# A state-space layer's decay rows: one tile of 32 partitions, copied to DRAM one group of heads at a time

## The chip, the cores and the metric

The kernel runs on one core of one Trainium2 chip. The metric is device time in microseconds (us); lower is better. The core has five engines with queues of their own, each of which takes its instructions in order: PE (matmuls), ACT (activations, copies), DVE (elementwise work), POOL (here masks and small adds) and SP, which issues nearly all DMAs.

## The reference

Two layers. Each is a half-step feed-forward part, a mixer, and a second half-step feed-forward part, with a layer norm behind each. The mixer of layer 0 is a bidirectional state-space scan over 512 tokens with 32 heads in 4 groups (8 heads of 64 channels each, state size 128); that of layer 1 is differential attention. The scan is what the change touches. In one direction, by chunks:

```python
def ssd_chunked(X, dt, A, Bm, Cm):
    Xc = (X * dt[..., None]).reshape(b, c, CHUNK, g, j, p)
    a = (dt * A).reshape(b, c, CHUNK, g, j).transpose(0, 3, 4, 1, 2)
    a_cs = jnp.cumsum(a, axis=-1)
    L = jnp.exp(segsum(a))                     # decay between two tokens of a chunk
    CB = jnp.einsum('bclgn,bcsgn->bgcls', Cc, Bc)
    y_diag = jnp.einsum('bgcls,bgjcls,bcsgjp->bclgjp', CB, L, Xc)
    ...
    y_off = jnp.einsum('bclgn,bcgjpn,bgjcl->bclgjp', Cc, states, jnp.exp(a_cs))
    return (y_diag + y_off).reshape(b, t, h, p)
```

For every head and direction this needs the cumulated decay of each token, once with tokens along the partitions (as the bias of an activation) and once with tokens along the free axis, the same row on all 128 partitions.

## The kernel before, in words

All matrices are float32, held as a rounded part and a rest (`hi`, `lo`), so that each product is three matmuls (`mm3`, line 176). Weights come from DRAM in units of 512 KB (`load`, line 99, four `raw` buffers in this layer), ACT rounds a unit (line 123), DVE takes the rest (line 124), and 24 matmuls of 128x512 use it. PE has work for nearly the whole span.

`ssm` (line 651) runs the state-space layer. It first projects group 0 (`win`: two units for B and C, four for x, four for z). Among these stands `dt_chain` (line 673), which makes the step sizes and cumulated decays of all heads: PE turns the cumulated values `cs` (tokens on partitions) into rows, one per head and direction, with four transposes of 64 columns (line 720), so that forward heads lie on partitions 0 to 31 and backward heads on 32 to 63 of one PSUM tile. ACT copies all 64 into `rows` (line 722) and writes the exponentials of one half of each direction to `rowe` (lines 724, 725).

A row must reach 128 partitions. That goes by way of DRAM: four DMAs on SP (line 729) write `rows` and `rowe` to `scr`, every row 16 times over (16 copies x 32 heads x 3 kinds x 512 tokens, 3.1 MB). Then, per head, `ssd_head` (line 819) reads them back with each of the 16 copies going to 8 partitions: `rw` (line 823, both directions' decays, 512 KB, two buffers) and `ch` (line 825, the exponentials, 256 KB, three buffers). POOL masks `rw` with four instructions per head (line 840). `ssd_mats` (line 845) then makes a head's decay matrix for one half of the tokens: four exponentials on ACT (lines 848 to 851), an add on POOL (854), a product on DVE (855). `ssd_out` (line 858) multiplies with it on PE (line 865).

The loop of a group (line 932) has 8 steps, here called s0 to s7: a pair of heads (0 and 1, 2 and 3, ...) times two halves of the tokens. A "block" below is the six matmul instructions of one step. Between steps stand units of the next group's projections, so that PE has something to do. `prepare(1)` (line 778; its first instruction on PE is line 783) follows group 0's last step.

The order on each queue is not that of the code: a scheduler places each instruction by its own estimate of when its inputs are there, so a change of a DMA's shape can move instructions on all engines. An instruction that has to wait stops what is behind it on its queue.

Of the kernel before, what the change touches and what calls it, by code (L numbers as in the profile page):

```python
# [9 lines left out]
F32 = mybir.dt.float32  # L10
F32R = mybir.dt.float32r
AF = mybir.ActivationFunctionType
ALU = mybir.AluOpType

P = 128
T = 512
# [6 lines left out]
NG = 4  # L23
# [23 lines left out]
def hybrid_trunk(tc, xT, cb, par, cst, adaw, wgu, wdn0, wdn1, wdn2, wdt, win, wso, wqk, wv, wao, dist_in, dtp, lam_in, out):  # L47
    nc = tc.nc
# [13 lines left out]
    def big(dt=F32, name="big"):  # L62
        return ap.tile([P, T], dt, tag="a", name=name)
# [4 lines left out]
    def acc(tag="acc"):  # L68
        return ps.tile([P, T], F32, tag=tag, name=tag, bufs=BANKS[tag])
# [7 lines left out]
    ident, ones = csts[:, 0, :], csts[:, 1, :]  # L77
# [573 lines left out]
    def ssm(n):  # L651
        u = next_u[0]
        sc = ExitStack()
        ep = sc.enter_context(tc.tile_pool(name="ep", bufs=2))
        dp = sc.enter_context(tc.tile_pool(name="dp", bufs=1, space=bass.MemoryType.DRAM))
# [5 lines left out]
        W = 256  # L661
        bias = ep.tile([P, 4, 64], F32, name="ssbias", bufs=1)
        dd = ep.tile([P, 4, 32], F32, name="dd", bufs=1)
        scr = dp.tile([16, 32, 3, T], F32, name="scr")

        def dt_proj():
            w = split(load(wdt, 512))
# [5 lines left out]
        def dt_chain(pd):  # L673
            dtT = tmp("dtT")
            nc.scalar.activation(dtT[:64], pd[:64], AF.Copy)
            pt = acc("ln")
            for i in range(4):
                nc.tensor.transpose(pt[:, i * 64 : (i + 1) * 64], dtT[:64, i * P : (i + 1) * P], ident[:64, :64])
            e1, e2, e3 = (ep.tile([P, T], F32, tag="E", name="E", bufs=NE) for _ in range(3))
            v, q, e, uu, lu = e1[:, :W], e1[:, W:], e2[:, :W], e2[:, W:], e3[:, :W]  # L680
            nc.vector.tensor_tensor(out=v, in0=pt[:, :W], in1=dtc[:, :W], op=ALU.add)
            nc.vector.scalar_tensor_tensor(out=q, in0=v, scalar=-1.0, in1=v, op0=ALU.mult, op1=ALU.max)
            nc.scalar.activation(e, q, AF.Exp, scale=-1.0)
            ea = e3[:, W:]
            nc.scalar.activation(ea, dtc[:, W:], AF.Exp)
            nc.vector.tensor_scalar(out=v, in0=v, scalar1=0.0, scalar2=None, op0=ALU.max)
            nc.vector.tensor_scalar(out=uu, in0=e, scalar1=1.0, scalar2=None, op0=ALU.add)
            nc.scalar.activation(lu, uu, AF.Ln)
            nc.vector.tensor_scalar(out=uu, in0=uu, scalar1=1.0, scalar2=None, op0=ALU.subtract)
            nc.vector.tensor_tensor(out=uu, in0=e, in1=uu, op=ALU.subtract)  # L690
            nc.vector.tensor_scalar(out=e, in0=e, scalar1=-0.5, scalar2=1.0, op0=ALU.mult, op1=ALU.add)
            nc.vector.tensor_tensor(out=uu, in0=uu, in1=e, op=ALU.mult)
            nc.vector.tensor_tensor(out=lu, in0=lu, in1=uu, op=ALU.add)
            nc.vector.tensor_tensor(out=v, in0=v, in1=lu, op=ALU.add)
            at = q
            nc.vector.scalar_tensor_tensor(out=at, in0=v, scalar=-1.0, in1=ea, op0=ALU.mult, op1=ALU.mult)
            nc.vector.tensor_scalar(out=v, in0=v, scalar1=1e-37, scalar2=None, op0=ALU.max)
            nc.scalar.activation(lu, v, AF.Ln)
            pcs = acc("ln")
            nones = tmp("nones")[:, :P]  # L700
            nc.gpsimd.memset(nones, -1.0)
            plan = {
                (0, 0): [(sgt, 0), (nones, 1)], (0, 1): [(sgt, 1)],
                (0, 2): [(sle, 2)], (0, 3): [(ones, 2), (sle, 3)],
                (1, 0): [(sge, 0), (ones, 1)], (1, 1): [(sge, 1)],
                (1, 2): [(slt, 2)], (1, 3): [(nones, 2), (slt, 3)],
            }
            for (dr, i), lst in plan.items():
                for k, (mk, j) in enumerate(lst):
                    nc.tensor.matmul(  # L710
                        pcs[:, i * 64 + dr * 32 : i * 64 + dr * 32 + 32], lhsT=mk,
                        rhs=at[:, j * 64 + dr * 32 : j * 64 + dr * 32 + 32],
                        start=k == 0, stop=k == len(lst) - 1,
                    )
            cs = tmp("cs")[:, :W]
            nc.scalar.activation(cs, pcs[:, :W], AF.Copy)
            nc.vector.tensor_tensor(out=bias.rearrange("p i h -> p (i h)"), in0=lu, in1=cs, op=ALU.subtract)
            pr = acc("ln")
            for i in range(4):
                nc.tensor.transpose(pr[:64, i * P : (i + 1) * P], cs[:, i * 64 : (i + 1) * 64], ident)  # L720
            rows = big(name="rows")
            nc.scalar.activation(rows[:64], pr[:64], AF.Copy)
            rowe = big(name="rowe")
            nc.scalar.activation(rowe[32:64, :W], pr[32:64, :W], AF.Exp)
            nc.scalar.activation(rowe[0:32, W:], pr[0:32, W:], AF.Exp)
            nc.scalar.activation(dd[:, 0:2, :], bias[:, 0:2, 0:32], AF.Exp)
            nc.scalar.activation(dd[:, 2:4, :], bias[:, 2:4, 32:64], AF.Exp)
            for j, a, b, src in ((0, 0, T, rows[0:32]), (1, 0, T, rows[32:64]), (2, 0, W, rowe[32:64]), (2, W, T, rowe[0:32])):
                nc.sync.dma_start(
                    scr[:, :, j, a:b].rearrange("r h x -> h r x"), src[:, a:b].unsqueeze(1).broadcast_to([32, 16, b - a])  # L730
                )

        last_in, last_exp = [None], [None]

# [83 lines left out]

        def ssd_head(h, Ct):

            src = scr[:, h].unsqueeze(1)
            rw = ep.tile([P, 2, T], F32, tag="rw", name="rw")
            nc.sync.dma_start(rw, src[:, :, 0:2].broadcast_to([16, 8, 2, T]))
            ch = ep.tile([P, T], F32, tag="ch", name="ch", bufs=3)
            nc.sync.dma_start(ch, src[:, :, 2].broadcast_to([16, 8, T]))
            nc.vector.tensor_tensor(out=ch, in0=ch, in1=Ct, op=ALU.mult)
            dx = ep.tile([P, 2, 2, P], F32, tag="dx", name="dx")
            f4 = rw[:, 0, :].rearrange("p (c o q) -> p c o q", c=2, o=2)
            b4 = rw[:, 1, :].rearrange("p (c o q) -> p c o q", c=2, o=2)
            for o, i_, fwd in (  # L830
                (f4[:, :, 0, :], f4[:, :, 0, :], True), (b4[:, :, 1, :], b4[:, :, 1, :], False),
            ):
                mask(o, i_, fwd)
            for o in range(2):
                mask(dx[:, :, o, :], (b4 if o == 0 else f4)[:, :, o, :], o == 1, inplace=False)
            return rw, ch, dx
# [75 lines left out]
        ln, shifting = LN(n), []  # L912
# [11 lines left out]
        for g in range(NG):  # L924
            xt, cbs, states, Ct = cur
            nbc, nxs = [], []
            first = units_z(g, zs[g])[len(zs[g]) :]
            if g < NG - 1:
                first = units_bc(g + 1, nbc) + units_x(g + 1, nxs) + first
            todo = first + ([lambda gg=g - 1: outp(gg)] * 4 if g > 0 else [])  # L930
            tot, done, batched = len(todo), 0, False
            for s in range(8):
                pr_, c = divmod(s, 2)
                ft = g * 4 + pr_
                if c == 0:
                    heads = [ssd_head(ft * 2 + hh, Ct) for hh in range(2)]
                    py = acc("mid")
                mats = [ssd_mats(ft * 2 + hh, c, heads[hh][0], heads[hh][2], cbs) for hh in range(2)]
                ssd_out(pr_, c, py, mats, [hd[1] for hd in heads], xt, states)
                if c == 1:  # L940
                    nc.vector.scalar_tensor_tensor(
                        out=xs[pr_], in0=xs[pr_], scalar=pc(C_D + ft), in1=py, op0=ALU.mult, op1=ALU.add
                    )
                if s == 0 and norm is not None:
                    rest = norm()
                if s == 2 and norm is not None:
                    yrs[g - 1] = rest()
                while done < tot - (2 if g == NG - 1 else 0) and done < (s + 1) * tot // 8:
                    todo[done]()
                    done += 1  # L950
                if done >= len(first) and not batched and (s >= 6 or done == tot):
                    batched = True
                    silu(zs[g] + nbc + nxs)
                    if g < NG - 1:
                        cur = prepare(g + 1, nxs, nbc)
            norm = (lambda g=g, xs=xs: gated_norm(g, xs, zs[g]))
            xs = nxs
# [314 lines left out]
```

## Time and profile before

| what | value |
|---|---|
| three runs | 2177.52, 2182.35, 2185.12 us (median 2182.35) |
| the profiled execution | 2177.95 us |
| its span, first to last instruction | 2176.1 us |
| mean granted TensorE clock | 0.992 |
| busy share of PE, DVE, ACT, POOL | 97%, 81%, 50%, 7% |
| state-space layer, from the decay chain on | about 400 to 780 us |
| the four writes of `scr` | issued 416.7 to 419.9 us |
| first step's first block on PE | 459.6 us |
| `prepare(1)` on PE | 512.6 us |

The profile gives times from the first instruction. A line of a timeline reads: start, length, engine, source line, operation, what it writes and reads, how many, and in square brackets how long the engine was idle before it and what ended that. "DMA to landing" is the time from a DMA's issue to its last byte's arrival. A window's row lists busy time per engine, then the granted TensorE clock, the busy share of the 16 DMA engines, and GB/s moved. [...]

### The profile page before, as it was taken

What the parts mean: (1) busy time and instruction counts of PE and PEld (TensorE: products, weight loads), DVE (VectorE), ACT (ScalarE), POOL (GpSimd) and SP (SyncE); (2) the same over time, 40 slices, a digit from 0 to 9 for tenths busy, and PEclk for the clock granted to TensorE, in tenths of its full rate; (3) what the DMA queues carried; (4) which work ended last, traced back from release to release, by engine and by line L of the source; (5) the groups of instructions that cost most, each with busy time, mean ns of one, the idle gap of its engine ahead of it and who ended that gap; (6) DMA issues with size and microseconds to landing.
All of it is one profiled execution on the core that took longest, in us unless ns stands there. A gap on an engine that the chain in (4) does not pass through costs nothing.

```text
span 2176.1 us, 34041 instructions
## 1 busy us (share of the span) xinstructions
PE 2120.5 (97%) x13206; PEld 1857.6 (85%) x13206; DVE 1765.4 (81%) x2934; ACT 1092.2 (50%) x1828; POOL 155.2 (7%) x258
## 2 busy tenths in 40 slices
PE   7999999999999998999999999999999999999997
PEld 6889899866777677989899989899988878989897
DVE  6979998556666688979988998997777888958696
ACT  4424354757656546434355534344766647524353
POOL 0000000034332310000000000000111100000000
PEclk9999999999999998999999999999999999999999
DMA  8853644464445413554533272733322212423231
GB/s 320 304 213 118 222 130 166 115 181 136 145 126 158 123 64 126 174 185 153 196 125 112 95 265 92 254 100 124 89 78 78 88 44 84 136 70 116 77 117 40
DMA packets 90082, 301.19 MB, mean 138 GB/s; under 512 B 10048, under 2 KB 13504, under 8 KB 89920
## 3 DMA queue, kind: packets, MB, share of 16 engines
q1 hardware_dynamic: 88384, 294.81, 41.3%
q0 software_dynamic: 1536, 4.20, 0.9%
q8 instruction: 104, 1.70, 0.3%
q14 instruction: 58, 0.48, 0.1%
HBM read 289.53 MB, written 5.24 MB: 135 GB/s over the span
## 4 chain that ended last, share of the span: by engine, by line
PE 84%; DVE 5%; issue 4%; ACT 3%; POOL 2%; DMA 2%; POOLq 0%; SPq 0%; ACTq 0%; DVEq 0%
PE acc L176 67%; PE mid L176 10%; PE mid L865 2%; DMA raw<-in_adaw 1%; PE mid L1033 1%; DVE raw L195 1%; POOL E L854 1%; PE ln L176 1%; PE ln L813 1%; DMA raw<-in_wdn 0%; ACT wh L123 0%; ACT p L1043 0%; PE ln L1055 0%; POOL dx L840 0%; PE ln L264 0%
## 5 line engine op out<-in xcount | busy, mean ns | idle before, releaser
L176 PE MATMUL acc<-hi,wh 128*128 128x256 f32 (+1 forms) x1576 | 526.9, 336 | 3.1 <-ACT hi L153 1.9
L176 PE MATMUL acc<-hi,wl 128*128 128x256 f32 (+1 forms) x1576 | 525.9, 334 | 0.0
L176 PE MATMUL acc<-lo,wh 128*128 128x256 f32 (+1 forms) x1576 | 525.6, 334 | 0.3 <-DVE lo L154 0.2
L176 PE MATMUL acc<-uh,wh 128*128 128x256 f32 (+1 forms) x1160 | 391.8, 338 | 0.2 <-ACT wh L123 0.2
L176 PE MATMUL acc<-ul,wh 128*128 128x256 f32 (+1 forms) x1160 | 390.5, 337 | 0.0
L176 PE MATMUL acc<-uh,wl 128*128 128x256 f32 (+1 forms) x1160 | 389.5, 336 | 0.0
L123 ACT ACTIVATE wh<-raw 128x1024 fp32r<-128x1024 f32 (+1 forms) x210 | 213.0, 1022 | 272.7 <-DMA raw<-in_wdn 95.9
L528 ACT ACTIVATE wh<-raw 128x1024 fp32r<-128x1024 f32 x198 | 209.1, 1059 | 254.1 <-DVE raw L538 121.8
L176 PEld LDWEIGHTS acc<-hi,wh 128*128 128x128 f32 x1576 | 297.9, 189 | 40.1 <-ACT hi L153 5.2
L176 PEld LDWEIGHTS acc<-lo,wh 128*128 128x128 f32 x1576 | 298.0, 189 | 31.8 <-DVE lo L154 1.9
L176 PEld LDWEIGHTS acc<-hi,wl 128*128 128x128 f32 x1576 | 298.0, 189 | 29.9 <-issue 0.5
L124 DVE TENSOR_TENSOR wl<-raw,wh 128x1024 fp32r<-128x1024 f32 (+1 forms) x210 | 248.0, 1184 | 47.6 <-ACT wh L123 46.7
L529 DVE TENSOR_TENSOR wl<-raw,wh 128x1024 fp32r<-128x1024 f32 x198 | 241.2, 1220 | 24.0 <-ACT wh L528 23.0
L176 PEld LDWEIGHTS acc<-uh,wh 128*128 128x128 f32 x1160 | 219.3, 189 | 29.6 <-issue 6.6
L176 PEld LDWEIGHTS acc<-ul,wh 128*128 128x128 f32 x1160 | 219.7, 189 | 24.9 <-issue 3.3
L176 PEld LDWEIGHTS acc<-uh,wl 128*128 128x128 f32 x1160 | 219.7, 189 | 23.9 <-issue 2.4
L538 DVE TENSOR_TENSOR raw<-raw 128x512 f32<-128x512 f32 x264 | 181.3, 689 | 4.7
L195 DVE SCALAR_TENSOR_TENSOR raw<-raw,cond 128x1024 f32<-128x1024 f32 x144 | 174.1, 1221 | 9.6 <-DMA raw<-in_adaw 9.4
L401 DVE SCALAR_TENSOR_TENSOR resid<-acc,gv,resid 128x512 f32<-128x512 f32 (+1 forms) x164 | 108.6, 667 | 71.1 <-PE acc L176 70.8
L341 POOL TENSOR_TENSOR rr<-vr,mhalf 128x2 f32<-128x2 f32 x12 | 9.5, 789 | 1512.9 <-DVE vr L337 1512.9
L176 PE MATMUL mid<-uh,wh 128*128 128x256 f32 (+2 forms) x332 | 99.6, 302 | 0.6 <-DVE up L570 0.6
L176 PE MATMUL mid<-uh,wl 128*128 128x256 f32 (+2 forms) x332 | 99.3, 299 | 0.0
(267 smaller groups left out, 3939.6 us busy)
## 6 DMA issues: line engine op xcount, KB each, us to landing
raw<-in_wgu SPq DMA_DIRECT2D x176, 512.0 KB, 4.0
raw<-in_adaw SPq DMA_DIRECT2D x144, 512.0 KB, 4.7
raw<-in_wdn SPq DMA_DIRECT2D x64, 448.0 KB, 4.0
raw<-in_win SPq DMA_DIRECT2D x40, 512.0 KB, 3.8
raw<-in_wdn SPq DMA_DIRECT2D x32, 512.0 KB, 4.7
rw<-scr SPq DMA_DIRECT2D x32, 512.0 KB, 5.5
ch<-scr SPq DMA_DIRECT2D x32, 256.0 KB, 3.6
raw<-in_wso SPq DMA_DIRECT2D x16, 512.0 KB, 3.6
```

Of the source, the lines that this page charges most:

```text
L123: nc.scalar.activation(hi[:, :n], raw, AF.Copy)
L124: nc.vector.tensor_tensor(out=lo[:, :n], in0=raw, in1=hi[:, :n].bitcast(F32), op=ALU.subtract)
L176: last = nc.tensor.matmul(o, lhsT=a, rhs=b, start=start and j == 0, stop=j == n - 1, skip_group_check=not start)
L195: nc.vector.scalar_tensor_tensor(out=raw, in0=raw, scalar=1.0, in1=cond, op0=ALU.mult, op1=ALU.mult, accum_out=mods[l][:, j : j + 1],)
L401: nc.vector.scalar_tensor_tensor(out=res[d][:, a:b], in0=pd[:, a:b], scalar=gvec[n][:, d : d + 1], in1=res[d][:, a:b], op0=ALU.mult, op1=A ...
L528: nc.scalar.activation(x[0], r, AF.Copy)
L529: nc.vector.tensor_tensor(out=x[1], in0=r, in1=x[0].bitcast(F32), op=ALU.subtract)
L538: nc.vector.tensor_tensor(out=o, in0=x, in1=y, op=ALU.add)
L813: nc.tensor.matmul(pst, lhsT=bt[:, i * P : (i + 1) * P], rhs=xd, start=o == 0, stop=o == 1)
L854: nc.gpsimd.tensor_tensor(out=dg, in0=dg, in1=dx[:, c], op=ALU.add)
L865: nc.tensor.matmul(py[hh * 64 : (hh + 1) * 64, cc], lhsT=lhs, rhs=rhs, start=k == 0, stop=k == 2)
L1033: nc.tensor.matmul(ss[m], lhsT=q[:, c], rhs=qks[h, 1][m], start=j == 0, stop=j == 1)
```

## The change

The rows go to one tile of 32 partitions, `rows` with head on the partition and three kinds of 512 along the free axis. For that, each direction is transposed by itself (eight transposes of 32 columns into two PSUM tiles), ACT copies the forward rows, DVE the backward ones, and ACT writes the exponentials into the third part. `scr` becomes four DRAM tiles of 16 x 8 x 3 x 512, one per group of eight heads, and each is written by one DMA whose source is the eight partitions of that group (`copy_rows`, 128 runs of 6 KB, 786 KB). The first copy is issued in `dt_chain`; those of groups 1, 2 and 3 are issued in group 0's loop, behind the reads of the first, second and third pair of heads. The bytes are the same in all.

```diff
-        scr = dp.tile([16, 32, 3, T], F32, name="scr")
+        scr = [dp.tile([16, 8, 3, T], F32, name=f"scr{g}") for g in range(NG)]
+        rows = ep.tile([32, 3, T], F32, name="rows", bufs=1)
...
-            pr = acc("ln")
-            for i in range(4):
-                nc.tensor.transpose(pr[:64, i * P : (i + 1) * P], cs[:, i * 64 : (i + 1) * 64], ident)
-            rows = big(name="rows")
-            nc.scalar.activation(rows[:64], pr[:64], AF.Copy)
-            rowe = big(name="rowe")
-            nc.scalar.activation(rowe[32:64, :W], pr[32:64, :W], AF.Exp)
-            nc.scalar.activation(rowe[0:32, W:], pr[0:32, W:], AF.Exp)
+            pr = [acc("ln") for _ in range(2)]
+            for dr in range(2):
+                for i in range(4):
+                    c = i * 64 + dr * 32
+                    nc.tensor.transpose(pr[dr][:32, i * P : (i + 1) * P], cs[:, c : c + 32], ident)
+            nc.scalar.activation(rows[:, 0, :], pr[0][:32], AF.Copy)
+            nc.vector.tensor_copy(rows[:, 1, :], pr[1][:32])
+            nc.scalar.activation(rows[:, 2, :W], pr[1][:32, :W], AF.Exp)
+            nc.scalar.activation(rows[:, 2, W:], pr[0][:32, W:], AF.Exp)
+            copy_rows(0)
...
-            for j, a, b, src in ((0, 0, T, rows[0:32]), (1, 0, T, rows[32:64]), (2, 0, W, rowe[32:64]), (2, W, T, rowe[0:32])):
-                nc.sync.dma_start(
-                    scr[:, :, j, a:b].rearrange("r h x -> h r x"), src[:, a:b].unsqueeze(1).broadcast_to([32, 16, b - a])
-                )
+        def copy_rows(g):
+            src = rows[g * 8 : (g + 1) * 8].rearrange("h j x -> h (j x)").unsqueeze(1)
+            nc.sync.dma_start(scr[g].rearrange("r h j x -> h r (j x)"), src.broadcast_to([8, 16, 3 * T]))
...
-            src = scr[:, h].unsqueeze(1)
+            src = scr[h // 8][:, h % 8].unsqueeze(1)
...
                     heads = [ssd_head(ft * 2 + hh, Ct) for hh in range(2)]
+                    if g == 0 and pr_ < NG - 1:
+                        copy_rows(pr_ + 1)
```

The scheduler's order changes with it. On SP, at the place where the rows are written and the first heads read, before (all copies of `scr` have one name; `rw` and `ch` are one head's reads, and the number tells the buffer's use):

```order
L729 DMA scr_3721<-rows_4070 32x16x512 x2
L729 DMA scr_3721<-rowe_4072 32x16x256 x2
L823 DMA rw_4294<-scr_3721 128x1x1024
L823 DMA rw_4312<-scr_3721 128x1x1024
L825 DMA ch_4296<-scr_3721 128x1x512
L825 DMA ch_4314<-scr_3721 128x1x512
L825 DMA ch_4444<-scr_3721 128x1x512
```

and, in the changed kernel, from the same place on (`scr0` to `scr3` are the four groups' tiles; the lines moved by three or five):

```order
L734 DMA scr0_3721<-rows_3725 8x16x1536
L734 DMA scr1_3722<-rows_3725 8x16x1536
L826 DMA rw_4299<-scr0_3721 128x1x1024
L828 DMA ch_4301<-scr0_3721 128x1x512
L826 DMA rw_4317<-scr0_3721 128x1x1024
L828 DMA ch_4319<-scr0_3721 128x1x512
L828 DMA ch_4450<-scr0_3721 128x1x512
L734 DMA scr2_3723<-rows_3725 8x16x1536
L826 DMA rw_4448<-scr0_3721 128x1x1024
L826 DMA rw_4466<-scr0_3721 128x1x1024
L828 DMA ch_4468<-scr0_3721 128x1x512
L828 DMA ch_4599<-scr0_3721 128x1x512
```

Group 1's copy stands ahead of the first read, group 2's ahead of the reads of heads 2 and 3. Behind the last row shown come group 3's copy, the `rw` reads of heads 4 and 5, one more `ch`, and only then the next weight units; before, three weight units stood right behind the last row shown.

On PE, at the end of step s1 in group 0 (line 865 before is 868 now; `mid` is the step pair's output, `E` a decay matrix, `acc` a projection), before:

```order
L865 MATMUL mid_4330<-ch_4296,st_4269 64x256
L865 MATMUL mid_4330<-ch_4314,st_4269 64x256
L176 MATMUL acc_4653<-uh_3534,wh_4649 128x512
L176 MATMUL acc_4653<-ul_3535,wh_4649 128x512
L176 MATMUL acc_4653<-uh_3534,wl_4650 128x512
```

and in the changed kernel at the same place:

```order
L868 MATMUL mid_4336<-ch_4301,st_4274 64x256
L868 MATMUL mid_4336<-ch_4319,st_4274 64x256
L868 MATMUL mid_4485<-E_4486,xt_4259 64x256
L868 MATMUL mid_4485<-E_4493,xt_4259 64x256
L868 MATMUL mid_4485<-E_4486,xt_4269 64x256
L868 MATMUL mid_4485<-E_4493,xt_4269 64x256
L868 MATMUL mid_4485<-ch_4450,st_4297 64x256
```

Where a projection stood behind s1, the next step's block stands now. The blocks of s0 to s4 follow each other without a projection between them. The 120 projection matmuls that stood between s1 and `prepare(1)` all stand behind s4: 24, s5, 24, s6, 24, s7, 48. Ahead of s0 nothing moved but the transposes.

## The prediction

> **What bounds the kernel now.** I read the page first, then PE's waits within the state-space layer, then PE's and SP's timelines around the place of the change, then the DMA rate there.
>
> ```profile
> PE 2120.5 (97%) x13206; PEld 1857.6 (85%) x13206; DVE 1765.4 (81%) x2934; ACT 1092.2 (50%) x1828; POOL 155.2 (7%) x258
> L123 ACT ACTIVATE wh<-raw 128x1024 fp32r<-128x1024 f32 (+1 forms) x210 | 213.0, 1022 | 272.7 <-DMA raw<-in_wdn 95.9
> L124 DVE TENSOR_TENSOR wl<-raw,wh 128x1024 fp32r<-128x1024 f32 (+1 forms) x210 | 248.0, 1184 | 47.6 <-ACT wh L123 46.7
> ```
>
> PE is busy for 97% of the span, so a change counts only by what it does to PE. The two rows under it are the splitting of a weight unit, 1.02 us on ACT and 1.18 on DVE. In the layer's loop (440 to 770 us), the longest entry among PE's waits is this one:
>
> ```profile
> PE mid L865 <- DVE E L855: 4.9, 2, 4.5
> ```
>
> 4.9 us in two waits. PE's timeline shows where, with the last projection ahead of s0, the blocks of s0 and s1, the first part of the block of s4, and `prepare(1)`:
>
> ```profile
> 458.11 0.39 PE L176 MATMUL acc<-uh,wh 128*128 128x512 f32 x1
> 458.34 0.39 PE L176 MATMUL acc<-ul,wh 128*128 128x512 f32 x1
> 459.56 1.08 PE L865 MATMUL mid<-E,xt 128*64 128x256 f32 x8
> 461.77 0.60 PE L865 MATMUL mid<-ch,st 128*64 128x256 f32 x4
> ...
> 478.10 0.39 PE L176 MATMUL acc<-uh,wh 128*128 128x512 f32 x1
> 483.00 1.08 PE L865 MATMUL mid<-E,xt 128*64 128x256 f32 x2 [4.51 <-DVE E L855]
> ...
> 512.64 0.66 PE L783 MATMUL ln<-csts,xc 128*128 128x128 f32 x4
> ```
>
> Projection matmuls follow each other every 0.23 us (458.11, 458.34), so the 120 between s1 and `prepare(1)` take 27.6 us. The blocks of s0 and s1 together run from 459.56 to 462.1, 1.3 us each. The one large stall is ahead of s4: PE has nothing from 478.5 to 483.0. What it costs beyond the 4.5 us is in the window's clock:
>
> ```profile
> 480.00:500.00 20.00, 16.86 (x66) 9.41 (x66) 13.50 (x19) 12.94 (x31) 11.03 (x19) 0.83 0.53 151
> ```
>
> 0.83 of the full clock over 20 us is 3.4 us lost. So the stall is worth about 8 us in all, and that is the most the change could win here.
>
> The stall comes by way of SP. Its queue, then the time to landing of the reads of head 2 (issued 450.6) and of heads 4 and 5 (465.7 and 466.3):
>
> ```profile
> 416.74 0.87 SPq L729 DMA_DIRECT2D scr<-rows  x2
> 417.65 4.64 SPq L729 DMA_DIRECT2D scr<-rowe  x2
> 428.88 2.99 SPq L823 DMA_DIRECT2D rw<-scr  x2
> 434.71 1.80 SPq L825 DMA_DIRECT2D ch<-scr  x3
> 436.56 2.67 SPq L99 DMA_DIRECT2D raw<-in_win  x3
> ...
> 463.61 1.92 SPq L99 DMA_DIRECT2D raw<-in_win  x3
> 465.69 1.63 SPq L823 DMA_DIRECT2D rw<-scr  x2
> ```
>
> ```profile
> L823 SPq DMA_DIRECT2D rw<-scr x1: 521/521/521, 450.6 to 450.6; - x1
> DMA to landing us min/median/max: 5.1/5.1/5.1
> L823 SPq DMA_DIRECT2D rw<-scr x2: 521/762/1003, 465.7 to 466.3; - x2
> DMA to landing us min/median/max: 12.0/12.5/13.1
> ```
>
> A read alone lands in 5.1 us; behind three weight units it takes 12.0 and 13.1. Head 5's landed at 466.3 + 13.1 = 479.4, and PE began s4 3.6 us later. Reads are served behind what was issued ahead of them on the queue. That matters most for this change, since it puts the copies of later groups ahead of reads.
>
> **The change part by part.** *Small edits.* The rows that bear on them:
>
> ```profile
> 414.98 1.05 PE L720 MATMUL ln<-csts,cs 128*64 128x128 f32 x4
> 417.14 0.37 ACT L725 ACTIVATE rowe<-ln 32x256 f32<-32x256 f32 x1
> 446.14 0.51 ACT L848 ACTIVATE E<-rw,ssbias 128x256 f32<-128x256 f32 x1
> 440.34 0.77 POOL L840 TENSOR_SCALAR_AFFINE_SELECT rw<-rw 128x256 f32<-128x256 f32 x2 [1.21 <-DMA rw<-scr]
> ```
>
> Eight transposes stand for four; the four took 1.05 us on PE, and half the columns may halve each, so between 0 and 1.05 us is added on PE's path: 0.5. ACT does the same three row writes (the last ended at 417.5), and DVE takes one copy of 512 columns, by ACT's 0.37 for 256 about 0.74 us; both lie beside projections. Were that cover gone, they would delay the first DMA by 0.7 us. `rows` being ready sets the first copy's issue: 417.6.
>
> *Earlier reads.* In the SP timeline the first `rw` is issued at 428.9, after the two writes of `rows`, and the first `ch` at 434.7. A first copy that lands sooner would bring these forward. It buys nothing by itself: head 1's first mask began at 440.34, and ACT started s0's exponentials only at 446.14, when it was through with `prepare(0)`; PE came to s0 at 459.56.
>
> *The copies.* This is the term that decides. How long does one copy take whose source is 8 partitions? The first old write, 1.05 MB from 32 partitions, by its landing, and the rates while writes of 2 KB runs (421 to 427), of 1 KB runs (427 to 431), reads alone (435 to 437) and weights (443 to 445) filled the queue, and while the kernel's last result went to DRAM from 128 partitions in 1 KB runs:
>
> ```profile
> L729 SPq DMA_DIRECT2D scr<-rows x1: 334/334/334, 416.7 to 416.7; - x1
> DMA to landing us min/median/max: 6.7/6.7/6.7
> ```
>
> ```profile
> 421.00:427.00 6.00, 6.00 (x29) 4.95 (x28) 2.41 (x4) 4.82 (x8) 0.00 (x0) 1.00 0.99 197
> 427.00:431.00 4.00, 4.00 (x21) 3.21 (x19) 1.99 (x3) 1.54 (x3) 0.00 (x0) 1.00 0.98 189
> 435.00:437.00 2.00, 2.00 (x13) 1.45 (x11) 0.69 (x1) 0.60 (x1) 0.00 (x0) 1.00 1.04 240
> 443.00:445.00 2.00, 2.00 (x9) 1.27 (x8) 1.74 (x3) 0.99 (x3) 0.00 (x0) 1.00 1.01 403
> 2172.00:2174.00 2.00, 0.00 (x0) 0.00 (x0) 0.19 (x1) 0.78 (x2) 0.00 (x0) 0.50 0.96 323
> ```
>
> All 16 DMA engines were busy in each (0.96 to 1.04), yet the rate is 197, 189, 240, 403 and 323 GB/s. Halving the run cost only 4%; going to DRAM isn't the limit either, since 128 partitions did 323. What the slow rows share is a source of 32 partitions. If the rate follows the partitions, 8 give a quarter, 49 GB/s, and a copy of 0.786 MB takes T = 16 us. The other end is the rate kept: T = 4 us. From 128 to 32 partitions the rate fell by 1.7, not by 4, and 1.7 once more would make T = 7; but 323 and 403 from as many partitions show that something else caps these, while at 32 partitions the run length hardly moved the rate. So I take 16, from the row nearest to the case (197, 2 KB runs, 32 partitions, the same target).
>
> [...]
>
> *The queue.* Before rw of head 5 can land, the new order puts on SP's queue all four copies, six `rw` and five `ch`. Sizes and landing of these and of a weight unit:
>
> ```profile
> rw<-scr SPq DMA_DIRECT2D x32, 512.0 KB, 5.5
> ch<-scr SPq DMA_DIRECT2D x32, 256.0 KB, 3.6
> raw<-in_win SPq DMA_DIRECT2D x40, 512.0 KB, 3.8
> ```
>
> That is 6 x 0.524 + 5 x 0.262 = 4.46 MB of reads: 18.6 us at the 240 GB/s of reads alone, 11.1 at the 403 of weights; I take 15. Four copies are 64. The landing of the first write leaves a fixed part of 6.7 - 1.05 MB/197 GB/s = 1.4. Their waits (for buffers, that is for ACT and PE on earlier heads) fall inside the time that the queue is still at work on a copy, so head 5 lands at X = 417.6 + 64 + 15 + 1.4 = 498.0.
>
> *What that does to PE.* The five blocks s0 to s4 stand together, so from s1 on PE has only blocks until head 5 is there. As before, s4 starts 3.6 us after the landing, and its block at a cold clock takes about twice 1.2: it ends at X + 6. Weights aren't late: their units are issued behind head 5's read, land about 3.8 us after it and want 1.02 + 1.18 of splitting, so the first is ready at about X + 6 too. Then 120 projection matmuls (27.6) and three blocks (3.9), and a cold clock's 3.4 again: `prepare(1)` starts at X + 41, against 512.6 before. So the change costs X - 471.6 = 26.4, and 0.5 for the transposes: 27. Behind `prepare(1)` no copy is left and PE is as full as it was; I book nothing there.
>
> Of the two waits above, the 4.5 us and its cold clock are not lost twice: they are in the 512.6.
>
> **Rivals.** *The copy isn't slow* (T up to 9). Then copies don't bind: head 4's and 5's reads are issued about when they were (after the exponentials of heads 2 and 3), now with no weight units ahead, and land in 5.1 us: X = 466.3 + 5.1 = 471.4, and the change costs 0.3. PE idles between the blocks instead of ahead of s4 alone, and gets it back behind s4. For it: full DMA engines at 189 and 197 might mean a limit of the engines, or of a source row sent 16 times, which would not scale with partitions. Against: 323 from 128 partitions. By the profiled execution 2178, by the median 2182. [...]
>
> *Faster.* With T = 4 the first copy lands at 423, the whole chain of heads moves up with it, and s4 is ready before PE gets there. Then the stall goes with its clock: -8, 2170. It decides if head 5 lands by about 466. Against: ACT's 446.14, which no copy moves.
>
> *The order alone costs.* Copies are fast, but weights behind head 5's read come after s4, and PE waits for them at a cold clock: 8 us at most by the stall it has now, 2186.
>
> *The change doesn't do what it says*: "behind the first reads" holds for groups 2 and 3 only; group 1's copy is ahead of the first read on SP. That is in the sum already.
>
> **How the numbers follow.** The sum stands against the profiled execution's 2177.95 us: 2177.95 + 27 = 2205. The median shown is 4.4 above that execution; half of this puts the forecast at 2207. Chances: slow copy 0.72, copy not slow 0.17, faster 0.05, order alone 0.05, something else 0.01. With T from 12 to 18 and reads of 11 to 18.6, X goes from 478 to 509.6, the cost from 7 to 38.5, the time from 2185 to 2221: the forecast's own range. 8 in 10 need part of the second case, so the low end goes to 2179, the high end to 2222. A measurement can tell about 0.3% (6.5 us) from no change: faster by more, 0.06; within, 0.16 (nearly all of the second case, a little of the fourth); slower, 0.78.
>
> **What would show it.** Right: the first copy lands 16 to 18 us after its issue, GB/s in 418 to 434 about 50, the first `rw` is issued at about 435, PE idles between blocks from 462 to 500, `prepare(1)` starts near 539, and the distance from there to the end is as before. Wrong: a copy that lands in under 11 us; reads that overtake copies (landing in 5 us while a copy is under way); `prepare(1)` before 520; or time given back behind it.

## The result, and the profile after

| | before | changed |
|---|---|---|
| median of the runs, us | 2179.93 (2176.78 to 2185.12, 4 runs) | 2202.66 (2197.85 to 2203.89, 4 runs) |
| profiled execution, us | 2177.95 | 2197.85 |
| its span, us | 2176.1 | 2196.1 |

The ratio is 1.0102, with a 95% interval of 1.0085 to 1.0119: the change costs about 22 us. The forecast was 2207.

The first line of the page to read is the busy time, since a change counts by what PE does.

```profile
PE 2119.8 (97%) x13210; PEld 1859.5 (85%) x13210; DVE 1768.3 (81%) x2935; ACT 1093.1 (50%) x1828; POOL 158.1 (7%) x258
```

PE's 2119.8 us of work are the 2120.5 of before; the span has grown by 20.0, so all of it is idle time. PE's waits between 400 and 800 us name it (line, what it waited for: us in total, times, longest), and PE's timeline shows where it lies. `E` is a decay matrix, made from a head's `rw`; L786 is `prepare(1)`, and L778 the batch of SiLU activations on ACT that writes the `xc` which `prepare(1)` reads.

```profile
PE mid L868 <- DVE E L858: 22.4, 4, 11.6
PE ln L786 <- ACT xc L778: 4.9, 1, 4.9
```

```profile
459.86 1.08 PE L868 MATMUL mid<-E,xt 128*64 128x256 f32 x8
...
475.21 1.12 PE L868 MATMUL mid<-E,xt 128*64 128x256 f32 x2 [11.56 <-DVE E L858]
...
492.37 2.05 PE L868 MATMUL mid<-E,xt 128*64 128x256 f32 x7 [10.04 <-DVE E L858]
...
494.52 1.17 PE L868 MATMUL mid<-ch,st 128*64 128x256 f32 x3
...
533.22 0.93 PE L786 MATMUL ln<-csts,xc 128*128 128x128 f32 x4 [4.90 <-ACT xc L778]
```

s0 starts when it did (459.86 against 459.56). Then there are holes of 11.6 us ahead of s2 and 10.0 ahead of s4, where before had one of 4.5, and a new one of 4.9 ahead of `prepare(1)`. That starts at 533.2 in place of 512.6, 20.6 us later, so all of the loss has come about by here. From there to the end of the span it is 1662.9 us, before 1663.5: nothing is given back.

The holes come from SP's queue. Its timeline (start, time of issuing, line), then the rate in four stretches (the last three columns are the granted clock, the busy share of the 16 DMA engines, and GB/s), then the landing of the reads of heads 4 and 5:

```profile
418.13 0.66 SPq L734 DMA_DIRECT2D scr<-rows  x2
434.87 0.63 SPq L826 DMA_DIRECT2D rw<-scr  x1
435.54 4.94 SPq L828 DMA_DIRECT2D ch<-scr  x1
...
449.23 0.48 SPq L734 DMA_DIRECT2D scr<-rows  x1
458.21 5.44 SPq L826 DMA_DIRECT2D rw<-scr  x2
...
466.90 0.48 SPq L734 DMA_DIRECT2D scr<-rows  x1
475.20 5.44 SPq L826 DMA_DIRECT2D rw<-scr  x2
```

```profile
422.00:426.00 4.00, 4.00 (x20) 3.30 (x19) 1.38 (x2) 3.28 (x7) 0.00 (x0) 1.00 0.47 49
430.00:434.00 4.00, 4.00 (x23) 3.27 (x22) 2.27 (x3) 2.97 (x5) 0.00 (x0) 1.00 0.46 49
...
436.00:438.00 2.00, 1.95 (x11) 1.22 (x9) 0.69 (x1) 0.58 (x1) 0.00 (x0) 1.00 0.90 179
438.00:440.00 2.00, 2.00 (x10) 1.46 (x9) 0.36 (x1) 1.09 (x2) 0.00 (x0) 1.00 0.49 53
```

```profile
L826 SPq DMA_DIRECT2D rw<-scr x2: 514/2432/4349, 475.2 to 476.3; - x2
DMA to landing us min/median/max: 11.1/11.6/12.0
```

A copy alone moves 49 GB/s, 16 us for its 0.786 MB, and the first `rw`, which waits for it, is issued 16.7 us behind it. The busy share of the 16 engines is 0.47 meanwhile, 7.5 engines on average. When reads are in the queue too (436 to 438), the share is 0.90 and the rate 179; in 438 to 440 they are back at 0.49 and 53. Head 5's read, issued at 476.3, lands at 488.3.

### The profile page after: what moved, and what is told of

The parts are those of the page before. It is cut to its first block, busy times and chain, and to the rows that moved or that the text cites. A ratio compares the mean times of both kernels' runs of the same rounds, so it can differ in the third digit from the quotient of the medians.

```text
span 2196.1 us, 34047 instructions
## 1 busy us (share of the span) xinstructions
PE 2119.8 (97%) x13210; PEld 1859.5 (85%) x13210; DVE 1768.3 (81%) x2935; ACT 1093.1 (50%) x1828; POOL 158.1 (7%) x258
## 4 chain that ended last, share of the span: by engine, by line
PE 77%; issue 8%; DVE 7%; POOL 3%; ACT 3%; DMA 2%; POOLq 0%; SPq 0%; ACTq 0%; DVEq 0%
PE acc L176 62%; PE mid L176 9%; PE mid L868 1%; DVE raw L195 1%; POOL E L857 1%; PE mid L1038 1%; PE ln L176 1%; DMA raw<-in_adaw 1%; POOL dx L843 1%; DMA raw<-in_wdn 1%; ACT p L1048 1%; DVE wl L529 0%; POOL rw L843 0%; DVE raw L538 0%; PE ln L327 0%
## 5 line engine op out<-in xcount | busy, mean ns | idle before, releaser
L176 PEld LDWEIGHTS acc<-hi,wh 128*128 128x128 f32 x1576 | 297.5, 189 | 39.3 <-ACT hi L153 4.9
```

What stands on the lines that cost most here:

```text
L176: last = nc.tensor.matmul(o, lhsT=a, rhs=b, start=start and j == 0, stop=j == n - 1, skip_group_check=not start)
```

## The experiments

The theory at this point: a copy takes 16 us because its eight source partitions are neighbours; four such copies stand ahead of head 5's read; and PE has five blocks in a row that wait for these reads. The rivals: the rate goes by the number of partitions, or by how many DMA engines are at work (a busy share of 0.47); the tile, or the DMA with rows of 6 KB, is itself slow; the order of the blocks costs the time; or what matters is the one queue.

### e1: spread rows, same order

Head 8g+k gets partition 4k+g (the columns are permuted on the way into `cs`), so that a group's copy reads eight partitions four apart. The order on every queue is the changed kernel's.

```
...
-            src = rows[g * 8 : (g + 1) * 8].rearrange("h j x -> h (j x)").unsqueeze(1)
+            src = rows[g:32:4].rearrange("h j x -> h (j x)").unsqueeze(1)
```

> The order on every queue is the changed kernel's, but a group's eight rows lie on partitions g, g+4, ... g+28 in place of eight neighbours. Theory (the rate of a copy goes by which partitions it reads: eight neighbours reach a quarter of what 32 reach): spread rows are copied at 98 to 197 GB/s, a copy of 0.786 MB takes 4 to 8 us and not 16, prepare(1) starts between 505 and 517, and the time is 2175 to 2187 against 2202.7 for the changed kernel. Rival 1 (the rate goes by the number of partitions or by the number of copies): 49 GB/s and 2200 to 2205 again. Rival 2 (the order of the five blocks costs the time, not the copies): fast copies, and still over 2195.

Measured: 2188.13 us, 1.0049 times before (1.0033 to 1.0065). The rate while the first two copies run:

```profile
421.00:422.00 1.00, 1.00 (x6) 0.84 (x5) 0.96 (x2) 0.70 (x1) 0.00 (x0) 1.00 0.47 197
422.00:423.00 1.00, 1.00 (x6) 0.81 (x6) 0.44 (x1) 0.53 (x1) 0.00 (x0) 1.00 0.47 197
```

That is the cleanest comparison of the study. Eight partitions, the same bytes, the same busy share of the DMA engines (0.47 in both): 49 GB/s from neighbours, 197 from partitions four apart. The number of partitions doesn't set the rate here, and how many engines are busy doesn't either. A copy takes 4 us, and about half of the change's 22 us are gone. But 10 us stay, just above what the theory allowed (2188.1 for 2187 at most), and PE shows them:

```profile
467.51 2.75 PE L873 MATMUL mid<-E,xt 128*64 128x256 f32 x7 [5.09 <-DVE E L863]
479.28 2.05 PE L873 MATMUL mid<-E,xt 128*64 128x256 f32 x7 [6.13 <-DVE E L863]
...
521.64 1.12 PE L791 MATMUL ln<-csts,xc 128*128 128x128 f32 x4 [5.40 <-ACT xc L783]
```

With quick copies there are still holes ahead of s2 and s4 and ahead of `prepare(1)`, which starts at 521.6 (the theory had 517 at most). So the theory is half of it, and the second rival, the order, may hold the rest, though it had put the time over 2195. e6 and e7 take this up.

### e2: the tile alone

All 32 heads go out in one DMA ahead of the reads; there are no later copies.

```
-            src = rows[g * 8 : (g + 1) * 8].rearrange("h j x -> h (j x)").unsqueeze(1)
-            nc.sync.dma_start(scr[g].rearrange("r h j x -> h r (j x)"), src.broadcast_to([8, 16, 3 * T]))
+            src = rows.rearrange("h j x -> h (j x)").unsqueeze(1)
+            nc.sync.dma_start(scr.rearrange("r h j x -> h r (j x)"), src.broadcast_to([32, 16, 3 * T]))
...
-                    if g == 0 and pr_ < NG - 1:
-                        copy_rows(pr_ + 1)
```

> The tile of 32 partitions as in the changed kernel, but all 32 heads go out in one DMA ahead of the reads, 3.15 MB. Theory (32 partitions give 197 GB/s): it takes 16 us, as the four writes of the kernel before did together; the first rw is issued at about 429 to 435, the blocks on PE stand as before, and the time is 2176 to 2186. Rival (the tile, its eight transposes or a DMA with long rows is itself slow): the one copy takes 25 us or more, or prepare(1) starts over 10 us later than 512.6, and the time is over 2190.

Measured: 2176.75 us, 0.9988 (0.9976 to 1.0000). The rate while the copy runs:

```profile
419.00:420.00 1.00, 1.00 (x6) 0.83 (x5) 1.00 (x1) 0.98 (x2) 0.00 (x0) 1.00 0.98 203
...
432.00:434.00 2.00, 2.00 (x9) 1.31 (x8) 0.69 (x1) 0.58 (x2) 0.00 (x0) 1.00 0.96 197
```

Here a busy share of 0.96 goes with the 197 GB/s that went with 0.47 in e1. The first `rw` is issued at 434.66, and `prepare(1)` starts at 510.07. The tile of 32 partitions, the eight transposes and the long rows cost nothing that can be measured. (The order on PE isn't quite that of the kernel before: in e2 projections stand among the blocks of s0 and s1 too. e6 below has the tile and the transposes in the order of before, and costs nothing either.) So the cost isn't in the tile, but in how it is copied out.

### e3: later copies on another queue

```
+            q = nc.sync if g == 0 else nc.scalar
-            nc.sync.dma_start(scr[g].rearrange("r h j x -> h r (j x)"), src.broadcast_to([8, 16, 3 * T]))
+            q.dma_start(scr[g].rearrange("r h j x -> h r (j x)"), src.broadcast_to([8, 16, 3 * T]))
```

> The copies of groups 1 to 3 are issued on ACT's queue, that of group 0 on SP's; rows stay on eight neighbours each. Theory (what costs is that reads stand behind slow copies on one queue): each later copy still takes about 16 us, but reads of heads 0 to 7 go past it, head 5 lands at 470 to 478 in place of about 488, and the time is 2178 to 2192. Rival (copies and reads share the DMA engines, whatever the queue): rw lands 15 us or more behind its issue while a copy is under way, and the time stays at 2197 or more.

Measured: 2220.1 us, 1.0196 (1.0176 to 1.0215): slower than the changed kernel. The theory missed and the rival held. ACT issues the copy of group 1 at 416.96, when SP issues that of group 0. The rate while the two run side by side, and DMA rows of three stretches of SP's and ACT's queues (KB each, us from issue to landing): reads issued at 434.5, at 475.6, and at 477.9 behind a copy that ACT issued at 477.5.

```profile
420.00:428.00 8.00, 8.00 (x38) 6.60 (x36) 0.69 (x1) 2.34 (x2) 0.00 (x0) 1.00 0.49 99
```

```profile
rw<-scr SPq DMA_DIRECT2D x1, 512.0 KB, 17.4
...
rw<-scr SPq DMA_DIRECT2D x1, 512.0 KB, 4.6
...
scr<-rows ACTq DMA_DIRECT2D x1, 768.0 KB
ch<-scr SPq DMA_DIRECT2D x2, 256.0 KB, 17.9
```

A read that meets a copy lands as late when the copy is on the other queue (17.4 and 17.9 us; 4.6 between copies). The other queue didn't take the reads past the copies. Two copies at once ran at a busy share of 0.49, where one alone had 0.47, yet together they moved 99 GB/s, twice what one does. So with one copy under way the engines weren't at their limit. Why a read lands so late beside a copy isn't shown.

PE's order differs in this kernel (projections moved ahead of `prepare(0)`), so its time doesn't weigh the queue alone. What it lost can be read from ACT's timeline and PE's: ACT stood still for 7.1 us for the first `rw`, with work of `prepare(0)` behind it, PE waited 12.8 us behind that and 13.3 us for the late `ch`.

```profile
451.90 1.28 ACT L852 ACT_TABLE_LOAD   x1 [7.11 <-DMA rw<-scr]
```

```profile
458.36 2.08 PE L817 MATMUL ln<-xd,bt 128*128 128x512 f32 x2 [12.82 <-DVE xd L813]
...
496.57 0.69 PE L869 MATMUL mid<-ch,st 128*64 128x256 f32 x1 [13.25 <-DVE ch L830]
```

### e4: the later copies doubled

```
...
+            if g:
+                nc.sync.dma_start(scx[g - 1].rearrange("r h j x -> h r (j x)"), src.broadcast_to([8, 16, 3 * T]))
```

> Each of the three later copies is issued twice on SP, the second into DRAM that nobody reads: 2.36 MB more. Theory (the copies on SP's queue are the cost, 16 us each, with nothing to hide them): three copies more are 48 us, those of groups 1 to 3 all ahead of what PE waits for, so prepare(1) starts 35 to 48 us later than 533.2 and the time is 2235 to 2252. Rival (the copies are covered by other waits, and the order is what costs): under 15 us more, up to 2217.

Measured: 2240.11 us, 1.0286 (1.0265 to 1.0308).

```profile
503.86 1.08 PE L871 MATMUL mid<-E,xt 128*64 128x256 f32 x2 [22.89 <-DVE E L861]
...
533.11 0.79 PE L176 MATMUL acc<-uh,wh 128*128 128x512 f32 x1 [20.96 <-ACT wh L123]
...
572.51 1.12 PE L789 MATMUL ln<-csts,xc 128*128 128x128 f32 x4 [5.66 <-ACT xc L781]
```

`prepare(1)` starts 39.3 us later than in the changed kernel, for three copies more. That is 13.1 us for a copy of 16: four fifths of each lie open, as the theory had it. It isn't the copies alone, though: on PE the block of s5 has moved up to the five others, ahead of 24 projections, and the weights are late too (20.96), as they stand behind the last copies on the queue.

### e6 and e7: all copies first, spread and neighbours

Both issue the four copies at once, ahead of the first read; e6 reads the spread rows of e1, e7 eight neighbours. Short of the transposes, PE's order is the kernel before's in both, with projections between the blocks, and from e6 to e7 no queue's order changes.

```
-            copy_rows(0)
+            for g in range(NG):
+                copy_rows(g)
...
-                    if g == 0 and pr_ < NG - 1:
-                        copy_rows(pr_ + 1)
```

> Spread rows as in e1, and all four copies issued at once ahead of the first read; the blocks on PE then stand between projections, as in the kernel before. e1 showed 197 GB/s for such a copy, yet cost 10 us. Theory (those 10 us are the price of the order with five blocks together): four copies of 4 us are through at about 434, prepare(1) starts between 508 and 516 and the time is 2173 to 2182. Rival (spread rows, or four DMAs of 8 rows, cost something by themselves): 2185 or more, as e1.

> Instruction for instruction the order of e6 on every queue, but each copy reads eight neighbouring partitions, as in the changed kernel. Theory (49 GB/s from eight neighbours, one copy behind the other): four copies take 64 us, to about 482; the first reads are through at about 486 to 492 in place of 440 to 446, s0 starts some 25 to 35 us later than in e6, and the time is 2200 to 2215. Rival (the order made most of the changed kernel's cost, and slow copies are covered): under 2190.

Measured: e6 2176.53 us, 0.9987 (0.9975 to 1.0000); e7 2206.0 us, 1.0120 (1.0100 to 1.0140). PE of e6, then of e7:

```profile
458.00 1.08 PE L874 MATMUL mid<-E,xt 128*64 128x256 f32 x8
...
494.12 0.62 PE L874 MATMUL mid<-E,xt 128*64 128x256 f32 x2 [2.14 <-DVE E L864]
509.30 0.60 PE L792 MATMUL ln<-csts,xc 128*128 128x128 f32 x4
```

```profile
484.08 2.74 PE L869 MATMUL mid<-E,xt 128*64 128x256 f32 x7 [25.20 <-DVE E L859]
...
537.35 0.60 PE L787 MATMUL ln<-csts,xc 128*128 128x128 f32 x4
```

Both came out as their theories had it. From e6 to e7 one thing differs, which partitions a copy reads (and, with it, the permuting of the columns, which e6 has and e7 hasn't: two instructions of 0.6 us instead of 0.4), and that is worth 29.5 us (28.1 at `prepare(1)`). The four kernels make a table:

| median, us (ratio to before) | blocks between projections | five blocks together |
|---|---|---|
| eight partitions four apart | e6: 2176.5 (0.9987) | e1: 2188.1 (1.0049) |
| eight neighbours | e7: 2206.0 (1.0120) | changed: 2202.7 (1.0102) |

Down a column, neighbours cost 29 us (1.0120 less 0.9987, of 2179) and 12 (1.0102 less 1.0049; 11.6 at `prepare(1)`). Along the upper row, later copies and the order that goes with them cost 12 to 13 us, with no slow copy in it (11.6 by the medians, 13.5 by the ratios). Along the lower row no difference is shown, as the intervals overlap: what the order costs, it seems to win back by letting the first reads through ahead of two of the four slow copies (s0 starts at 459.86 there, at 484.08 in e7). So the two causes don't simply add. By way of e1, about 12 of the change's 22 us go with the slow copies and 10 with the order; by way of e7, the slow copies cost all of it. e6's last line shows one thing that goes with the order: no wait at all ahead of `prepare(1)`, where e1 had 5.40.

### e5: copies one group ahead

```
-                    if g == 0 and pr_ < NG - 1:
-                        copy_rows(pr_ + 1)
+                    if pr_ == 3 and g < NG - 1:
+                        copy_rows(g + 1)
```

> Copies from eight neighbours as in the changed kernel, but one group ahead only: group 0's ahead of the first read, group 1's behind the reads of heads 0 and 1, group 2's among the reads of group 1. Theory (each copy holds up the reads behind it for its 16 us, and before prepare(1) there are now two, not four): the copy of group 1 runs from about 438 to 454, reads of heads 2 and 3 land 5 to 10 us later than in the kernel before, and the time is 2180 to 2192. Rival (a slow copy costs its 16 us in any place, since nothing covers it): four copies still, 2198 or more.

Measured: 2182.19 us, 1.0016 (1.0004 to 1.0027). On SP, group 1's copy is issued at 437.84, group 2's at 495.36, group 3's at 544.39:

```profile
437.84 0.49 SPq L734 DMA_DIRECT2D scr<-rows  x1
460.64 1.91 SPq L826 DMA_DIRECT2D rw<-scr  x2
...
495.36 0.48 SPq L734 DMA_DIRECT2D scr<-rows  x1
499.79 5.47 SPq L826 DMA_DIRECT2D rw<-scr  x2
```

The copies are as slow as ever (the first `rw` is issued at 434.63, 16.8 us behind the first copy), but they are issued 20 to 58 us apart, and PE has projections between the blocks. Of four copies' 64 us only 3.4 show; the first 16 are no more than the four writes of the kernel before took (3.1 MB at 197 GB/s). The time is in the theory's range. So slow copies can be covered; what wasn't covered, in the changed kernel and in e7, is four of them ahead of one group's reads.

### e9 and e10: a third buffer for rw

e9 is the kernel before with `bufs=3` for `rw`. e10 adds that to e2, with the third row of a head in a tile and a DMA of its own.

```
-            rw = ep.tile([P, 2, T], F32, tag="rw", name="rw")
+            rw = ep.tile([P, 2, T], F32, tag="rw", name="rw", bufs=3)
```

> The kernel before with a third buffer for rw, so that reads of heads are issued earlier, ahead of weight units. Theory (in the kernel before, the only large stall is the 4.5 us ahead of s4, with 3.4 us of lost clock behind it, and it comes from rw landing 12 to 13 us behind three weight units): the stall goes and the time is 2169 to 2175. Rival (PE then waits for something else, the weights or the SiLU batch): 2176 to 2182.

> The gains of e2 and e9 together: rows of all 32 heads on 32 partitions and written out at once, in two DMAs (two rows of a head, then the third), with a third buffer for rw; the reads and the blocks stand as in e9. Theory (the two gains are of one kind, the wait of the first blocks for reads, and the 16 us of writing are the same): prepare(1) starts at 507 to 511 and the time is 2172 to 2178, no better than e9 by more than 0.2%. Rival (the gains add): 2168 to 2172.

Measured: e9 2176.41 us, 0.9984 (0.9973 to 0.9995); e10 2177.06 us, 0.9990 (0.9981 to 0.9999). PE of e9, then of e10:

```profile
477.26 0.86 PE L865 MATMUL mid<-E,xt 128*64 128x256 f32 x5 [2.07 <-DVE E L855]
...
508.78 0.66 PE L783 MATMUL ln<-csts,xc 128*128 128x128 f32 x4 [2.19 <-ACT xc L775]
```

```profile
512.70 0.66 PE L788 MATMUL ln<-csts,xc 128*128 128x128 f32 x4 [2.38 <-ACT xc L780]
```

The 4.5 us stall of the kernel before shrinks to 2.1, and 2.2 come back ahead of `prepare(1)`. e9's time is the one that its rival gave: PE then waits for the SiLU batch. The gains of e2, e6 and e9, some 3 us each by the ratios, are at the edge of what can be measured, and e10 shows no sign that those of e2 and e9 add; its time is in the theory's range, and its `prepare(1)` starts at 512.70, later than the 507 to 511 of the theory. All four are ahead of the changed kernel by 1%, and of the one before by 0.2% at most, with intervals that reach to 1.0000 for e2 and e6.

## Why the prediction was right, step by step

The sign and the mechanism came out, and the size too: 2202.7 for 2207. That it came so near is in part luck, as two errors of the sum went against each other: head 5 landed 9.7 us earlier than booked, and from there to `prepare(1)` it took 3.9 us longer.

- **The small edits.** The first copy is issued at 418.1, forecast 417.6, and e2, which has all of them, is no slower than before. Right.
- **T = 16 us.** Right: 49 GB/s in 422 to 426 and 430 to 434, as worked out from a quarter of 197. What stood behind it was the author's estimate that 8 of 32 partitions give a quarter. e1 shows that as put it doesn't hold: eight partitions gave all 197 once they stood four apart. The forecast held because "eight" and "neighbours" went together. The rates measured are 49 GB/s from eight neighbours, 99 from two such copies at once (e3), 197 from eight that stand four apart (e1) and 197 from 32 (e2). Why neighbours are copied more slowly isn't shown.
- **A limit of the engines.** That full DMA engines at 189 and 197 GB/s might mean a limit of the engines was an argument for the rival. The busy share set no rate here: 49, 99 and 197 GB/s all went through at 0.46 to 0.49.
- **Reads between the copies.** This is the term that was mis-sized: 15 us, with 1.4 fixed, gave X = 498.0. Head 5 landed at 476.3 + 12.0 = 488.3. From the first issue, four copies take it to 418.1 + 64 = 482.1, so only 6.2 are left for the 16.4 booked. Reads between copies were reckoned as if a copy held the whole queue. The busy share with a copy alone was 0.47, and reads went on beside it: 179 GB/s at a share of 0.90 in 436 to 438, and 53 again behind that.
- **From X to `prepare(1)`.** s4 started at X + 4.1 (3.6 forecast) and ended at 495.7, X + 7.4 (X + 6): its block took 3.3 us, for the 2.4 booked, at a granted clock of 0.50 (492.4 to 495). Behind it 120 projections and three blocks took to 533.2 - 4.9 = 528.3, that is 32.6 us for 27.6 + 3.9, so of the cold clock's 3.4 only 1.1 are left; the granted clock was 0.91 in 495 to 500 and 1.00 from there to 528. (The 3.9 was a little short: the blocks of s0 and s1 end at 461.77 + 0.60 = 462.4 and not at 462.1, which makes 1.4 us a block.) Then came the 4.9 us for the SiLU batch (L778), which nothing in the sum had. Together X + 44.9 for X + 41, and 533.2 for 539.
- **Nothing behind `prepare(1)`.** Right: 1662.9 us to the end, 1663.5 before.
- **The rival "the copy isn't slow".** Its price was wrong, though it didn't come to be: 2178 by the profiled execution, 2182 by the median. e1 is that case, and it took 2188.1. Head 5 landed at 475.1 (465.2, and 9.9 to land) and not at 471.4, as the fourth copy is issued at 463.65, right ahead of the two reads; that is 3.7 us. And there is the wait of 5.4 ahead of `prepare(1)`, whose cause stays open (below). 3.7 + 5.4 = 9.1, and `prepare(1)` started 9.0 later than before. PE didn't get its idle time back behind s4, as the rival had it. "The order alone costs" was nearer, with up to 8 us, but by another way than its late weights.

```profile
463.65 0.68 SPq L739 DMA_DIRECT2D scr<-rows  x1
464.50 2.31 SPq L831 DMA_DIRECT2D rw<-scr  x2
```

```profile
L831 SPq DMA_DIRECT2D rw<-scr x2: 515/1070/1626, 464.5 to 465.2; - x2
DMA to landing us min/median/max: 8.7/9.3/9.9
```

**What stays open.** The wait for the SiLU batch ahead of `prepare(1)` is 4.9, 5.4, 5.2 and 5.7 us in the changed kernel, e1, e3 and e4, and 2.2 and 2.4 in e9 and e10; it isn't there in the kernel before, e2, e5, e6 and e7. So five blocks together aren't what it takes: e3, e9 and e10 have projections among theirs. The changed kernel's trace shows that a read is late here too, by way of POOL and ACT. POOL's mask waits for `rw`, and ACT's last exponential ahead of the batch waits for the mask:

```profile
526.67 1.68 POOL L843 TENSOR_SCALAR_AFFINE_SELECT rw<-rw 128x256 f32<-128x256 f32 x2 [0.92 <-DMA rw<-scr]
...
528.74 0.40 ACT L853 ACTIVATE dx<-dx,ssbias 128x128 f32<-128x128 f32 x1 [2.28 <-POOL dx L843]
```

All six kernels have such a wait on ACT, of 2.3 to 3.0 us, right ahead of the batch, and 48 projections in one stretch ahead of `prepare(1)`; the others have no such wait, and at most 43. Which of the two makes it, no run took by itself.

## What to carry to other kernels

When a transfer is cut into pieces by partitions, look at which partitions a piece has: here eight neighbours were copied at a quarter of the rate of 32 (49 GB/s), eight that stood four apart at the full one (197). Count what stands ahead of the first read that somebody waits for, on every queue, as in e3 a slow copy delayed reads on the other queue just as well (17.4 and 17.9 us to landing, 4.6 between copies). And a change of DMAs can move the order of the matmuls: compare that order first, and make a kernel that has the new order without the new cost.

## What was not expected of the hardware

- Behind a slow copy the issuing itself takes long on SP: 4.94 us for one read at 435.54, with copies at 49 GB/s under way; in e6, with quick ones, 1.31 for the same read. In e7 the first of three weight units took 4.70 too, but the second, at 463.21 and with copies still under way, only 0.36:

```profile
454.27 4.70 SPq L99 DMA_DIRECT2D raw<-in_win  x1
...
463.21 0.36 SPq L99 DMA_DIRECT2D raw<-in_win  x1
```

  In the changed kernel the read behind that one was issued at 440.52, right where the 4.94 us ended: what is behind a slow issue on SP's queue isn't even issued meanwhile. Why it takes so long isn't shown.
- The DMA engines moved 197 GB/s from eight spread rows at a busy share of 0.47 (e1), and 197 from 32 rows at 0.96 (e2). So a busy share near 1 didn't mean here that the engines set the rate.
